# First-head row maxima among the last projections, and later memory units, in a two-layer attention trunk

## The chip, the cores and the metric

The kernel runs on one core of a Trainium2 chip. The metric is the time of one execution on the device in microseconds (us), the median of several runs; less is better. One execution was recorded by the hardware profiler, and the views of it are what is read below. The engines: PE (TensorE) multiplies, DVE (VectorE), ACT (ScalarE) and POOL (GpSimd) do the elementwise work, SP issues most loads. "bank" is one of the eight 512-column banks of PSUM, the only place PE writes to.

## The reference

A decoder trunk of two layers over 2048 tokens of width 1024. Layer A mixes tokens by multi-head latent attention, layer B by attention with forget gates; both have 12 causal heads and 4 heads that read 256 memory tokens.

```python
for i in range(DEPTH):                                   # A, then B
    hn = rms_norm(h, norm_pre[i])
    k_m, v_m = split(rms_norm(mem, mem_norm) @ w_mem_kv[i])
    if i % 2 == 0:
        c_q, c_kv, k_r, q_m, gate = split(hn @ w_in_a)
        main = mla(rms_norm(c_q) @ w_q_up, rms_norm(c_kv) @ w_kv_up, rope(...))   # causal softmax
    else:
        q, k, v, f_logit, q_m, gate = split(hn @ w_in_b)
        main = fox(q, k, v, cumsum(log_sigmoid(f_logit + b_f)))                  # causal softmax
    mem_out = softmax(q_m @ k_m.T * MEM_DIM**-0.5) @ v_m
    y = concat([main, mem_out]) * silu(gate)
    h = h + rms_norm(y @ w_out[i], norm_post[i])
```

## The kernel before

Every operand is split into a high and a low part, and a product is the sum of two or three matmuls of parts (`mm3`, L255). Intermediate results (q, k, v, gate, y) go through DRAM.

**The order of the program** (`trunk_kernel`): the projections of A; the up-projection `up_a` in four groups of 512 tokens; A's attention; `out_proj(0)`; `proj_b`, whose two last chunks (k and q of heads 8 to 11) run over the token groups in the order 1, 2, 3, 0; B's attention; `out_proj(1)`. `up_a` and `proj_b` are generators: at a `yield` they hand over to code that prepares the attention, so that this is placed among their last groups. Up to the attention the order on each engine comes from a list scheduler that goes by priority (`high_priority` puts work ahead) and by what its own model of the chip says is ready. `attention` itself is written out by hand, step by step (`manual_schedule`).

**Units and steps.** The attention is cut into units: one head and 512 queries (`Unit`, g = 0 to 3). A unit of a causal head needs first its row maxima (`max_closures`: q by k on PE at L1580, each 512 columns reduced on DVE at L1551 or, at the diagonal, L1583; 4 (g + 1) of them), then their negatives in a row of q (`nm`, `nm_row`, L1600 and L1601). Its steps then each make 1024 columns of logits (L1709), their exp on ACT (L1651), a high part on ACT (L202) and a low part on POOL (L224; on DVE where the step is narrow), and later the value products (L1725, 24 a step) and the division (`finish`, L1733 and L1738). A memory unit has two maxima (L1562) and one step.

**Memory units.** There are 16 in each layer. `MEM_EARLY` of them (6 in A, 8 in B) run among the last projections (`att_start`, `run_early`), `MEM_FIRST` (4, 4) at the head of the stream, and the rest follow, two per head (`MEM_AFTER`). The first causal head's k and v are loaded by `att_head`; all its maxima are made in the stream.

**The stream's planner** (`run_units`) keeps a list `maxq` of all maxima in order of units and, ahead of each step, lets out as many as a target in columns allows, at most `AHEAD` = 5 units ahead; half of them stand ahead of the step's logits on PE.

**Slots.** SBUF is cut into slots (A0 to A8, R0 to R4, S, G, Q), and a slot's next tenant waits until the last use of the one before. In `proj_b` the normalised input of group 1 lies in A4 and A5, of group 2 in A7 and A1, of group 3 in A2 and A8, of group 0 in A3 and A0. B's q of even heads lies in A3, of odd heads in A0. `up_a` stages its results in three tiles (`up_split`, L809 stores them) while its last group runs, and its banks are 4 and 7.

**The output projection** (`out_proj`): `z_prep` loads gate (L1195) and y (L1196) of 128 tokens, multiplies them on POOL (L1200), transposes on PE (L1204) and splits; the product is at L1229.

## Time and profile before

| | us |
|---|---|
| median of 3 runs | 2886.47 |
| lowest and highest run | 2885.28, 2890.05 |
| the profiled execution | 2885.39 |
| its span, first to last instruction | 2883.7 |

In the views, "out<-in" names tiles by the slots they lie in (bA is any of A0 to A8), and L255 is line 255 of the kernel. A stretch's PEclk is the clock granted to TensorE as a share of 2.4 GHz; 0.50 is its lower level, 1.2 GHz. A matmul's end is modelled, so busy times of neighbouring matmuls overlap slightly and distances between starts are the better price. A wait is put under the instruction that waited, behind the arrow what it waited for.

### The profile page before, as it was taken

The numbers are of one execution on the slowest core, as the hardware profiler recorded it, in microseconds if no ns is written. First come the engines' busy times: TensorE is split into PE (matmuls) and PEld (weight loads), VectorE is DVE, ScalarE is ACT, GpSimd is POOL, SyncE is SP. The second block draws the span as 40 slices with busy tenths as digits, with TensorE's granted clock in tenths as the row PEclk, the third lists the DMA queues.
The fourth block names the chain that finished last, engine by engine and source line by source line (L and its number), as shares of the span: only waits on it lengthen the run. The fifth ranks groups of instructions, "written<-read, shape, count | busy, mean of one in ns | idle before, by whom it ended". The sixth has DMA issues, their size and how long they took to land. (4 is left out here: it accounts for less than half of the span.)

```text
span 2883.7 us, 58600 instructions
## 1 busy us (share of the span) xinstructions
PE 2789.8 (97%) x24017; PEld 2379.9 (83%) x24017; DVE 1563.8 (54%) x3358; ACT 1323.0 (46%) x1867; POOL 1251.2 (43%) x838
## 2 busy tenths in 40 slices
PE   7999999879999999999999999999999999999998
PEld 6789998657888888878888997999767788887787
DVE  7522215467777777745463325310268788887343
ACT  4322123237778788852141010111137788888311
POOL 2110123346677777772101002310037788888431
PEclk9999999979999999999999999999979999999999
DMA  5343447763433343255443223861454454465453
GB/s 186 125 140 100 133 146 264 229 204 93 106 74 88 76 100 93 55 190 190 146 156 118 76 82 121 291 225 61 132 149 113 116 134 123 112 171 170 147 175 117
DMA packets 260933, 398.42 MB, mean 138 GB/s; under 512 B 24793, under 2 KB 140521, under 8 KB 260521
## 3 DMA queue, kind: packets, MB, share of 16 engines
q1 hardware_dynamic: 180112, 255.21, 31.4%
q10 hardware_dynamic: 79016, 138.27, 13.3%
q8 instruction: 189, 3.10, 0.5%
q0 software_dynamic: 1536, 1.18, 0.3%
q14 instruction: 80, 0.65, 0.1%
HBM read 238.13 MB, written 156.47 MB: 137 GB/s over the span
## 5 line engine op out<-in xcount | busy, mean ns | idle before, releaser
L224 POOL TENSOR_TENSOR bA<-bA,bA 128x1024 f16<-128x1024 f32 (+5 forms) x277 | 507.8, 1844 | 293.9 <-ACT bA L202 219.5
L255 PE MATMUL banks<-bR,bA 128*128 128x256 f32 (+3 forms) x4437 | 549.1, 286 | 1.1 <-DVE bQ L507 0.6
L255 PEld LDWEIGHTS banks<-bR,bA 128*128 128x128 f32 x4437 | 540.7, 188 | 6.5 <-ACT bG L505 0.9
L255 PE MATMUL banks<-bA,bR 128*128 128x512 f32 (+2 forms) x2208 | 514.6, 390 | 6.9 <-ACT bS L823 4.2
L1709 PE MATMUL banks<-bA,bA 96*128 96x512 f32 (+13 forms) x1820 | 483.9, 377 | 0.3 <-ACT bA L1651 0.2
L255 PEld LDWEIGHTS banks<-bA,bR 128*128 128x128 f32 x2208 | 403.4, 191 | 93.3 <-ACT bS L823 5.4
L1651 ACT ACTIVATE bA<-banks 128x1024 f32<-128x1024 f32 (+1 forms) x414 | 370.7, 895 | 182.9 <-PE banks L1709 156.9
L1551 DVE TENSOR_REDUCE mx<-banks 128x1 f32<-128x512 f32 x576 | 387.8, 685 | 108.3 <-PE banks L1580 105.6
L202 ACT ACTIVATE bA<-bA 128x1024 f16<-128x1024 f32 (+5 forms) x400 | 336.5, 848 | 95.8 <-DMA qrs<-bA 22.0
L1709 PEld LDWEIGHTS banks<-bA,bA 96*128 96x128 f32 (+3 forms) x1820 | 327.5, 193 | 43.1 <-ACT bA L1651 0.9
L1580 PE MATMUL banks<-bA,bA 76*128 76x512 f32 (+5 forms) x868 | 317.3, 406 | 17.6 <-DVE bA L1601 4.9
L209 POOL TENSOR_SCALAR bR<-bR 128x1024 fp32r<-128x1024 f32 (+3 forms) x50 | 61.5, 1230 | 410.8 <-PE banks L255 360.1
L1583 DVE CUSTOM_DVE_ANT_0 bA<-banks,bA 128x128 bf16<-128x128 f32 (+3 forms) x384 | 186.6, 486 | 76.7 <-PE banks L1580 66.1
L1229 PE MATMUL banks<-bA,bA 128*128 128x512 f32 x960 | 226.6, 392 | 0.0
L1725 PEld LDWEIGHTS <-bA 128*128 128x128 f16 x5928 | 198.9, 99 | 28.9 <-issue 16.5
L1229 PEld LDWEIGHTS banks<-bA,bA 128*128 128x128 f32 x960 | 178.6, 188 | 36.1
L1580 PEld LDWEIGHTS banks<-bA,bA 76*128 76x128 f32 (+1 forms) x868 | 164.2, 196 | 50.5 <-DVE bA L1601 7.6
L1709 PE MATMUL banks<-bR,bA 128*128 128x512 f32 (+6 forms) x620 | 201.6, 391 | 0.9 <-DVE bR L1601 0.9
L224 POOL TENSOR_TENSOR bR<-bR,bR 128x1024 f16<-128x1024 f32 (+2 forms) x74 | 159.9, 2161 | 81.7 <-ACT bR L202 49.5
L1200 POOL TENSOR_TENSOR bA<-bA 128x512 f32<-128x512 f32 x64 | 102.4, 1622 | 207.8 <-DMA bA<-gs 195.1
L224 POOL TENSOR_TENSOR bR<-bA,bR 128x1024 f16<-128x1024 f32 (+2 forms) x76 | 154.7, 2038 | 67.4 <-ACT bR L202 31.0
L505 ACT ACTIVATE bG<-banks 128x256 f32<-128x256 f32 x128 | 49.1, 385 | 277.2 <-PE banks L255 197.2
(228 smaller groups left out, 3638.7 us busy)
## 6 DMA issues: line engine op xcount, KB each, us to landing
bA<-qbs SPq DMA_DIRECT2D x65, 256.0 KB
bA<-in_x_dram SPq DMA_DIRECT2D x32, 512.0 KB
gs<-bG ACTq DMA_DIRECT2D x128, 128.0 KB
bA<-gs SPq DMA_DIRECT2D x32, 512.0 KB
bA<-ys SPq DMA_DIRECT2D x32, 512.0 KB
bA<-h SPq DMA_DIRECT2D x28, 512.0 KB
ks<-bA ACTq DMA_DIRECT2D x24, 512.0 KB
qs<-bA ACTq DMA_DIRECT2D x24, 512.0 KB
```

The costliest lines, as they stand in the source:

```text
L202: nc.scalar.activation(out, in_, AF.Copy, scale=scale)
L209: nc.gpsimd.tensor_scalar(out, in_, scale, 0.0, op0=ALU.mult, op1=ALU.add)
L224: e.tensor_tensor(out=out, in0=in_, in1=hi, op=ALU.subtract)
L255: nc.tensor.matmul(out, lhsT=a, rhs=b, start=start and i == 0, stop=stop and i == n - 1)
L1200: nc.gpsimd.tensor_tensor(out=gt[:, hs], in0=gt[:, hs], in1=yt[:, hs], op=ALU.mult)
L1229: nc.tensor.matmul(ps[:, ns], lhsT=a, rhs=b[:, ns], start=c == 0 and j == 0, stop=c == KC - 1 and j == 2)
L1551: nc.vector.tensor_reduce(out=to, in_=ps, axis=AX.X, op=ALU.max, negate=negate)
L1580: nc.tensor.matmul(ps, lhsT=q[0:qr, t * P:(t + 1) * P], rhs=k[0:kr, x:x + w], start=True, stop=True)
L1583: nc.vector.tensor_tensor_reduce(out=ap["mj"].next()[:, 0:w], in0=ps, in1=K.mqk[:, G - w:G], scale=1.0, scalar=-3.0e38, op0=ALU.add, op1=A ...
L1651: nc.scalar.activation(pf[:, 0:w], ps[:, 0:w], AF.Exp, scale=self.scale, bias=LOGP)
L1709: nc.tensor.matmul(ps[:, o:o + bw], lhsT=k[0:kr, (self.k0 + kt) * P:(self.k0 + kt + 1) * P], rhs=q[0:qr, q0:q0 + bw], start=i == 0 and not ...
L1725: nc.tensor.matmul(self.pv[:, t, 0:n], lhsT=p[:, o:o + P], rhs=v[:, kv, a:a + n], start=self.first, stop=False, skip_group_check=True)
```

## The change

It does six things.
- Early memory units: 6 to 2 in A, 8 to 4 in B. Units at the head of the stream: 4 to 0 in A, 4 to 2 in B; of B's two the maxima are made early too (`MEM_READY`). The others, 14 in A and 10 in B, stay two per head in the stream.
- The first causal head's maxima of g = 0 and 1 in A and of all four g in B are made in `att_head`, among the last projections, with their q loads (`q_row`, or `q_dma` in A) and the mask (`max_mask`). The planner counts them as done.
- In `proj_b` the yields come after the first and the third of the four last groups (before: after the second and the third), `att_head` before `att_start`, and two banks, 4 and 7, serve from the second group on (before: six banks, then three for the last two groups). Slots of B move to fit: head 0's k and v in A4 and A5, the memory's in A7, A1, A2 and A8, q of even heads in A6, of odd heads in A3.
- At the stream's end, when no maxima are left, the low part of a step is made on DVE right behind its high part.
- In `out_proj` the gate products of the first two tiles run on DVE, and the gain is loaded after the first tile's gate and y.
- q of the next two units is asked for ahead of every step.

```diff
--- before.py
+++ after.py
-MEM_EARLY = {0: 6, 1: 8}
-MEM_FIRST = {0: 4, 1: 4}
+ROWS_AHEAD = 600
+MEM_EARLY = {0: 2, 1: 4}
+ROWS_EARLY = {0: 2, 1: NG}
+MEM_READY = {0: 0, 1: 2}
+MEM_FIRST = {0: 0, 1: 2}
...
         prep(len(jobs) - 1)
         for g in (1, 2, 3, 0):
-            if g == 0:
+            if g == 2:
                 yield
-            elif g == 3:
+                env = (stp, self.banks(4, 7), hn)
+            elif g == 0:
                 yield
-                env = (stp, self.banks(4, 7, 1), hn)
             for k, (_, ms) in enumerate(last):
                 self.run_chunk(env, ms, W[len(jobs) - 2 + k], g)
...
+    def att_place(self, l):
+        if self.l != l:
+            self.ap, self.k_t, self.v_t, self.yt, self.l = {}, {}, {}, {}, l
+            self.ap["pm"], self.ap["ps"], self.ap["pv"] = self.banks(*((2, 3) if l == 0 else (1, 2, 3))), self.banks(5, 6), self.banks(0)
+        return self.ap
...
-            km, ph, pa, ymp, qq = B("A4", r=True), B("A5"), B("A7"), B("A1"), B("R4", r=True)
+            km, ph, pa, ymp, qq = B("A7", r=True), B("A1"), B("A2"), B("A8"), B("R4", r=True)
...
         first = [self.mem_units.pop(0) for _ in range(MEM_EARLY[l])]
-        for u in first:
+        ready = self.mem_units[:MEM_READY[l]]
+        for u in first + ready:
             u.q = ap["qq"].next()
         with self.tc.high_priority(offset=EARLY_AHEAD):
-            run_early(mem, first)
+            run_early(mem, first, ready)
...
-    def att_head(self):
-
-        l, B = self.l, self.box
-        self.v0 = B("A2" if l == 0 else "A8")
-        self.kv_place("0", B("A1" if l == 0 else "A2", r=True), self.v0)
+    def att_head(self, l):
+
+        B = self.box
+        self.att_place(l)
+        self.v0 = B("A2" if l == 0 else "A5")
+        self.kv_place("0", B("A1" if l == 0 else "A4", r=True), self.v0)
...
         self.head0 = Head(self, l, "mla" if l == 0 else "fox", 0)
         for _, f, _ in self.head0.prep():
             f()
+        self.ready = {}
+        if l:
+            self.qb_t = {}
+            self.qb_place("A6", 0)
+        mb = self.v0 if l else self.ap["mb"]
+        self.max_mask(mb, mb)
+        with self.tc.high_priority(offset=ROWS_AHEAD):
+            for g in range(ROWS_EARLY[l]):
+                u = self.ready[g] = Unit(self, l, self.head0, 0, g)
+                if l:
+                    u.q_row()
+                else:
+                    u.q = self.ap["qq"].next()
+                    u.q_dma()
+                for f, _ in u.max_closures():
+                    f()
+                u.nm()
+                u.nm_row()
+
...
+    def qb_place(self, slot, odd):
+
+        nb = DH + FB
+        box = self.box(slot, r=True)
+        for g in range(NG):
+            t = self.qb_t[g + NG * odd] = box.tile([nb, 2, G], F32R, name=f"qb{g}")
+            ind = self.v0.tile([FB, G], F32, name="ind")
+            self.nc.gpsimd.memset(ind, 1.0)
+            for lo_b, hi_b in ((-(NR + 2 * g), 0), (0, NR + 1 + 2 * g)):
+                self.nc.gpsimd.affine_select(out=ind, in_=ind, compare_op=ALU.is_ge, fill=0.0, base=lo_b + hi_b,
+                                             pattern=[[0, G]], channel_multiplier=1 if lo_b else -1)
+            self.nc.vector.tensor_copy(t[DH:nb], ind[:, None, :].to_broadcast([nb - DH, 2, G]))
...
-        self.kv_place("1", B("A3" if l == 0 else "A6", r=True), yb if l == 0 else B("Q"))
+        self.kv_place("1", B("A3" if l == 0 else "A0", r=True), yb if l == 0 else B("Q"))
...
+            self.qb_place("A3", 1)
...
         units = [mu.pop(0) for _ in range(min(MEM_FIRST[l], len(mu)))]
         for h, hd in enumerate(heads):
             for g in range(NG):
-                units.append(Unit(self, l, hd, hd.h, g))
+                units.append(self.ready[g] if h == 0 and g in self.ready else Unit(self, l, hd, hd.h, g))
...
-            late = mid + [later("A4", q1, k) for k in range(4)]
+            late = mid + [later("A7", q1, k) for k in range(4)]
...
-        zb, gb, xp = (B("A1", r=True), B("A2"), B("A8")) if l == 0 else (B("A1", r=True), B("A3"), B("A4"))
+        zb, gb, xp = (B("A1", r=True), B("A2"), B("A8")) if l == 0 else (B("A8", r=True), B("A3"), B("A7"))
...
-        gain = xp.tile([P, D], F32, name="ogain")
-        self.bcast_row(gain, i["norm_post"][l])
...
-                nc.gpsimd.tensor_tensor(out=gt[:, hs], in0=gt[:, hs], in1=yt[:, hs], op=ALU.mult)
+                (nc.vector if t < 2 else nc.gpsimd).tensor_tensor(out=gt[:, hs], in0=gt[:, hs], in1=yt[:, hs], op=ALU.mult)
...
         nxt = z_prep(0)
+        gain = xp.tile([P, D], F32, name="ogain")
+        self.bcast_row(gain, i["norm_post"][l])
...
                 o.pv_steps([(s, box)])
             o.finish()
-    for u in objs[:3]:
+    both = objs + ready
+    for u in both[:3]:
         u.q_dma()
-    for u in objs[:2]:
+    for u in both[:2]:
         rows(u)
     for k, u in enumerate(objs):
-        if k + 3 < len(objs):
-            objs[k + 3].q_dma()
-        if k + 2 < len(objs):
-            rows(objs[k + 2])
+        if k + 3 < len(both):
+            both[k + 3].q_dma()
+        if k + 2 < len(both):
+            rows(both[k + 2])
...
+        if o.has_row:
+            at += sum(c for _, c in o.max_closures())
+            maxq.extend(late)
+            late.clear()
+            continue
...
+    done = sum(need[u] for u, o in enumerate(objs) if o.has_row)
...
-            if u > main and not (st["done"] + c <= target and u <= main + AHEAD):
+            if objs[u].hd.idx > cur[main] + 1 or u > main and not (c <= target and u <= main + AHEAD):
...
+        q_ahead(u + 2, u)
         close()
-        todo = advance(u, min(t * rate + lead, RUNUP * (t + 4 * G) + need[0]))
+        todo = advance(u, min(t * rate + lead, RUNUP * (t + 4 * G) + need[0] + done))
...
-        o.flow(s, box)
+        o.flow(s, box, st["k"] == len(maxq) and not todo)
         if before:
             before[0].flow_lo(before[1])
         before = None
+        if st["k"] == len(maxq) and not todo:
+            o.flow_lo(box)
+            box["dve"] = False
...
+    def q_row(self):
+
+        K, h, g = self.K, self.h, self.g
+        if self.mx_ops:
+            return
+        kb, nb = self.hd.kt[1], DH + FB
+        qb = self.qb = K.qb_t[g + NG * (h % 2)]
+        K.load_r(qb[0:DH], K.qbs[h // 2][(h % 2) * DH:(h % 2) * DH + DH, :, g * G:(g + 1) * G])
+        self.mx_ops = ((qb[:, 0], nb), (kb, nb))
+        self.nmrow, self.at = qb[DH:DH + NR, 1], DH
...
         nc.scalar.activation(pf[:, 0:w], ps[:, 0:w], AF.Exp, scale=self.scale, bias=LOGP)
         K.hi("act", ph[:, 0:w], pf[:, 0:w])
-        if w > G:
+        box["dve"] = w <= G or last
+        if not box["dve"]:
             K.lo("pool", pl[:, 0:w], pf[:, 0:w], ph[:, 0:w])
 
     def flow_lo(self, box):
         w = box["w"]
-        if w <= G:
+        if box["dve"]:
             self.K.lo("dve", box["pl"][:, 0:w], box["pf"][:, 0:w], box["ph"][:, 0:w])
...
     next(pb)
+    K.att_head(1)
+    next(pb)
     K.att_start(1)
-    next(pb)
-    K.att_head()
     drain(pb)
     K.attention()
```

## Rows read from the trace of the kernel before

**Rows 1.** The page: busy time, share of the span and instructions.

```profile
PE 2789.8 (97%) x24017; PEld 2379.9 (83%) x24017; DVE 1563.8 (54%) x3358; ACT 1323.0 (46%) x1867; POOL 1251.2 (43%) x838
```

**Rows 2.** Stretches: window, length, busy by engine (instructions), PEclk, DMA share, GB/s.

```profile
550.00:610.00 60.00, 48.62 (x263) 37.02 (x261) 34.61 (x53) 20.97 (x34) 22.12 (x22) 0.94 0.80 252
610.00:660.00 50.00, 36.72 (x182) 26.19 (x183) 33.00 (x74) 17.89 (x24) 18.14 (x15) 0.56 0.47 133
...
1100.00:1200.00 100.00, 99.51 (x1239) 83.30 (x1236) 73.29 (x164) 80.12 (x100) 77.70 (x42) 1.00 0.33 82
1254.00:1262.00 8.00, 4.42 (x97) 3.73 (x94) 3.10 (x4) 2.42 (x5) 6.27 (x5) 1.00 0.83 301
2127.00:2172.00 45.00, 39.34 (x215) 28.07 (x214) 37.04 (x77) 17.96 (x21) 19.27 (x17) 0.58 0.52 132
2172.00:2310.00 138.00, 131.47 (x1682) 106.24 (x1681) 105.33 (x247) 109.24 (x120) 104.38 (x50) 0.96 0.44 113
2400.00:2500.00 100.00, 98.73 (x1314) 80.90 (x1311) 83.49 (x194) 87.27 (x99) 84.63 (x40) 1.00 0.47 125
2654.00:2687.00 33.00, 25.98 (x358) 20.97 (x355) 5.61 (x9) 22.62 (x26) 30.75 (x17) 0.84 0.61 224
```

**Rows 3.** PE's waits, 550 to 660: waiter, releaser, us, times, longest.

```profile
PE banks L1562 <- DMA bA<-qms: 5.6, 3, 3.6
PE banks L1709 <- ACT bR L1691: 4.9, 1, 4.9
...
PE banks L1580 <- DMA bA<-qrs: 2.6, 1, 2.6
```

**Rows 4.** ACT's waits, 550 to 645, the longest.

```profile
ACT bA L202 <- DMA qrs<-bA: 15.0, 3, 7.2
```

**Rows 5.** PE in order of time: start, us, line, shape, count.

```profile
2113.21 0.40 PE L1709 MATMUL banks<-bA 128*128 128x512 f32 x1
...
2114.37 1.55 PE L255 MATMUL banks<-bA,bR 128*128 128x512 f32 x6
...
2117.59 5.01 PE L255 MATMUL banks<-bA,bR 128*128 128x512 f32 x21
2122.44 0.39 PE L1709 MATMUL banks<-bR,bA 128*128 128x512 f32 x1
```

**Rows 6.** SP in order of time, first v loads of A.

```profile
602.97 10.87 SPq L1458 DMA_DIRECT2D bA<-vs  x4
```

**Rows 7.** A stretch of B's projections, and a DVE group in it.

```profile
2036.00:2128.00 92.00, 92.00 (x517) 71.33 (x516) 32.36 (x55) 23.06 (x35) 13.85 (x14) 1.00 0.49 147
...
L224 DVE TENSOR_TENSOR bA<-bA,bA 128x512 f16<-128x512 f32 x6 | 4.2, 693 | 11.0 <-ACT bA L202 11.0
```

**Rows 8.** DVE: the maxima of the whole span; two copies in order of time.

```profile
L1551 DVE TENSOR_REDUCE mx<-banks 128x1 f32<-128x512 f32 x576 | 387.8, 685 | 108.3 <-PE banks L1580 105.6
...
2139.36 3.22 DVE L1108 CAST bA<-bA 12x1024 fp32r<-12x1024 f32 x2
```

**Rows 9.** PE's waits, 2127 to 2310, the longest.

```profile
PE banks L1580 <- DMA bA<-qbs: 4.1, 2, 2.6
```

**Rows 10.** The stream's end in B, in order of time.

```profile
2654.10 4.25 POOL L224 TENSOR_TENSOR bA<-bA,bA 128x1024 f16<-128x1024 f32 x2 [0.64 <-POOL bG L224]
2659.29 2.51 POOL L1200 TENSOR_TENSOR bA<-bA 128x512 f32<-128x512 f32 x2 [0.94 <-DMA bA<-ys]
...
2664.10 1.02 ACT L1651 ACTIVATE bA<-banks 128x1024 f32<-128x1024 f32 x1 [3.36 <-POOL bA L224]
2665.15 1.06 ACT L202 ACTIVATE bA<-bA 128x1024 f16<-128x1024 f32 x1
...
2648.87 1.63 PE L1725 MATMUL banks<-bQ,bA 128*128 128x65 f16 x48
```

**Rows 11.** DVE in order of time, the same shape twice.

```profile
664.93 0.57 DVE L224 TENSOR_TENSOR bQ<-bA,bG 128x256 f16<-128x256 f32 x1
...
2684.55 1.81 DVE L224 TENSOR_TENSOR bA<-bA,bA 128x256 f16<-128x256 f32 x1 [13.04 <-ACT bA L202]
```

More of the change, by code (lines that the diff above doesn't have):

```diff
@@ L197, in __init__ @@
         self.owed = 0.0
+        self.l = None
     def hi(self, eng, out, in_, scale=1.0):
@@ L1032, in att_start @@
         ap["qq"] = Turn(*(Later(lambda b=b, k=k: b.tile([P, 2, G], F32R, name=f"qq{k}")) for k, b in enumerate(qqs)))
-        ap["ymp"], ap["sp"] = ymp, sp
+        ap["ymp"], ap["sp"], ap["mb"] = ymp, sp, pa
         ap["ym"] = Turn(*(ymp.tile([P, 4, 2 * DH], F32, name=f"ym{k}") for k in range(4)))
         ap["vrm"] = Turn(vrp.tile([P, MEMH * NMEM // P, DH], F32, name="vrm"))
-        ap["pm"], ap["ps"], ap["pv"] = self.banks(2, 3), self.banks(5, 6), self.banks(0)
-        self.l, self.yt = l, {}
         self.k_ones("m")
@@ new lines, in max_mask @@
+    def max_mask(self, mb, jb):
+        mqk = self.mqk = mb.tile([P, G], BF16, name="mqk")
+        self.ap["mj"] = Turn(jb.tile([P, G], BF16, name="mj"))
+        self.nc.gpsimd.memset(mqk, 0.0)
+        self.nc.gpsimd.affine_select(out=mqk[:, G - P:G], in_=mqk[:, G - P:G], compare_op=ALU.is_ge, fill=NEG, base=0,
+                                     pattern=[[-1, P]], channel_multiplier=1)
+    def qb_place(self, slot, odd):
[9 more added lines that the diff above has]
+            self.nc.vector.tensor_copy(t[DH:nb], ind[:, None, :].to_broadcast([nb - DH, 2, G]))
@@ L1084, in attention @@
         gb, fewer = B("G"), None
-        mb, jb = (v0, yb) if l == 0 else (ap["sp"],) * 2
-        mqk = self.mqk = mb.tile([P, G], BF16, name="mqk")
-        ap["mj"] = Turn(jb.tile([P, G], BF16, name="mj"))
-        nc.gpsimd.memset(mqk, 0.0)
-        nc.gpsimd.affine_select(out=mqk[:, G - P:G], in_=mqk[:, G - P:G], compare_op=ALU.is_ge, fill=NEG, base=0,
-                                pattern=[[-1, P]], channel_multiplier=1)
         more = (v0, yb, gb, ap["sp"]) if l == 0 else (ap["ymp"], gb, v0, v0)
@@ L1098, in attention @@
             ap["qa"] = Turn(*(Later(lambda k=k: qa.tile([P, G], F32R, name=f"qa{k}")) for k in range(4)))
-            qb = B("A3", r=True), B("A0", r=True)
-            self.qb_t = [qb[j // NG].tile([nb, 2, G], F32R, name=f"qb{j}") for j in range(2 * NG)]
-            for g in range(NG):
-                ind = v0.tile([FB, G], F32, name="ind")
-                nc.gpsimd.memset(ind, 1.0)
-                for lo_b, hi_b in ((-(NR + 2 * g), 0), (0, NR + 1 + 2 * g)):
-                    nc.gpsimd.affine_select(out=ind, in_=ind, compare_op=ALU.is_ge, fill=0.0, base=lo_b + hi_b,
-                                            pattern=[[0, G]], channel_multiplier=1 if lo_b else -1)
-                for j in (g, g + NG):
-                    nc.vector.tensor_copy(self.qb_t[j][DH:nb], ind[:, None, :].to_broadcast([nb - DH, 2, G]))
+            self.qb_place("A3", 1)
         heads = [self.head0] + [Head(self, l, "mla" if l == 0 else "fox", h) for h in range(1, HEADS)]
@@ L1137, in attention @@
             ts = early if u.kind == "mem" or l == 0 and u.hd.idx < MORE_Q else late if k > free else mid
-            u.q = min(ts, key=lambda q: used.get(q, -1))
+            u.q = u.q or min(ts, key=lambda q: used.get(q, -1))
             used[u.q] = k
         W = self.W = {}
-        slots = ("A4", "A4", "A5", "A5", "A7", "A7", "R0", "S") if l == 0 else ("R2", "R3", "R4", "S", "A2", "A2", "A8", "A8")
+        slots = ("A4", "A4", "A5", "A5", "A7", "A7", "R0", "S") if l == 0 else ("R2", "R3", "R4", "S", "A4", "A4", "A5", "A5")
         wb = {}
@@ L1211, in out_proj @@
         nxt = z_prep(0)
+        gain = xp.tile([P, D], F32, name="ogain")
+        self.bcast_row(gain, i["norm_post"][l])
+        if l == 0:
+            self.xbox = B("A6")
+            gpre = self.gpre = self.xbox.tile([P, D], F32, name="ogpre")
+            self.bcast_row(gpre, i["norm_pre"][1])
         for t in range(NT):
@@ L1255, in out_proj, with run_early @@
                 yield
-def run_early(mem, objs):
+def run_early(mem, objs, ready):
     K = mem.K
@@ L1297, in run_units @@
     n = len(objs)
-    maxq, late = [], []
+    maxq, late, at = [], [], 0
     for u, o in enumerate(objs):
+        if o.has_row:
[3 more added lines that the diff above has]
+            continue
         cols = 0
         for f, c in o.max_closures():
-            maxq.append((u, f, c))
+            at += c
+            maxq.append((u, f, at))
             cols += c
@@ L1307, in run_units @@
         late.append((u, o.nm_row, 0))
-    maxq.append(late.pop())
+    maxq.extend(late)
     steps = [(u, s, max(b[1] + b[3] for b in s)) for u, o in enumerate(objs) for s in o.steps()]
-    need = [0] * n
-    for u, f, c in maxq:
-        need[u] += c
+    cur = [1] * n
+    for u, o in enumerate(objs):
+        cur[u] = o.hd.idx or cur[max(u, 1) - 1]
+    need = [sum(c for _, c in o.max_closures()) for o in objs]
     width = [0] * n
@@ L1336, in run_units @@
     aux.sort(key=lambda x: (x[0], x[1]))
-    st = dict(k=0, done=0, dma=0)
+    st = dict(k=0, dma=0)
     def run_aux(t, head=-1):
@@ L1367, in advance @@
             todo.append(f)
-            st["done"] += c
             st["k"] += 1
@@ L1639, in main_closures, with flow @@
         return out
-    def flow(self, blocks, box):
+    def flow(self, blocks, box, last):
         K, nc, ap = self.K, self.K.nc, self.K.ap
@@ L1753, in trunk_kernel @@
     next(up)
-    K.att_head()
+    K.att_head(0)
     drain(up)
```

28 lines of the change are left out of this document (10 added, 18 removed).

## The prediction

> **What bounds the kernel now.** First the page's line of busy times: PE is busy for 97% of the span [rows 1], so look for what PE loses, not for what the other engines do. The second view is the table of stretches: for each stretch the PE busy time times the granted clock is the work at 2.4 GHz that was done in it, and the length less that is loss. In the two attention streams almost nothing is lost: 100 - 99.51 = 0.5 us of 100 in layer A, 100 - 98.73 = 1.3 us of 100 in layer B [rows 2]. There PE itself sets the pace, and work put into a stream costs what it takes on PE. The loss sits at the seams [rows 2]:
> - 550 to 610, last group of A's up-projection: 60 - 48.62 x 0.94 = 14.3 us.
> - 610 to 660, the way into A's stream: 50 - 36.72 x 0.56 = 29.4 us.
> - 1254 to 1262, A's stream into the output projection: 8 - 4.42 = 3.6 us.
> - 2127 to 2172, the way into B's stream: 45 - 39.34 x 0.58 = 22.2 us.
> - 2172 to 2310, B's first head and a half: 138 - 131.47 x 0.96 = 11.8 us.
> - 2654 to 2687, the end of B's stream: 33 - 25.98 x 0.84 = 11.3 us.
>
> Together 92.6 us. The product takes the mean clock for the busy time, so each is an estimate. Most of the two big ones is clock: granted 0.56 and 0.58, that is mostly the 1.2 GHz level, after PE had begun to wait. Everything the change does is at these seams.
>
> **The price of a memory unit.** The third view is PE's order of time late in B's projections. One cycle from one unit to the next lasts 2122.44 - 2113.21 = 9.23 us and holds 27 projection matmuls [rows 5]; the run of 21 takes from 2117.59 to 2122.44, so 0.231 us each and 6.24 us for the 6 + 21. The unit itself is 9.23 - 6.24 = 3.0 us of PE. In A eight units leave the seam (six early and four first become two and none), in B six (eight and four become four and two): 24 and 18 us of PE. All of it comes back in the streams at 3.0 us each, at full clock; nothing is saved by the move as such. What counts is whether the loss at the seam shrinks.
>
> **A, the way into the stream (29.4 us).** PE waits here for q of memory units (5.6 us), for q rope of the first head (2.6 us), and 4.9 us for an exp [rows 3]; the exp stood on ScalarE behind a copy that waited for a staging tile's store to land, as the 15.0 us of such waits show [rows 4]. After: the first head's first two units bring their four q loads, their 12 maxima and two negated-row steps forward beside the last q projections, behind the k loads of that head on SP. The two DMA waits go. The staging wait stays, because the three staging tiles stay: 4.9 us. A shorter stretch at 1.2 GHz behind it: 10 us, costing 5. A new burst: the planner lets about nine maxima into the first step, 9 x 0.685 = 6.2 us of VectorE [rows 8] against 9 x 0.231 = 2.1 us of PE with three banks between them: 3 us after the logits of that step are taken off. Left 13, bounds 5 (no pause, so no fall of the clock) and 24 (only the waits for memory q go). Gain 16.
> Against it: the units that leave were also filler. Between 550 and 610 PE waits for banks behind the same stores, and four early units of 3.0 us stood in those holes or would have to: 0 to 12 us of new holes; the 12 maxima, 12 x 0.231 = 2.8 us, fill some. I take 3, near the low end, because 48.62 of 60 us were busy, so most units displaced projection work rather than holes. First values: the v loads of the first head are issued from 602.97 on, 10.87 us long [rows 6], while the stream would now reach its first value product near 620; that can cost up to 8 us and is inside the upper bound. **A net: 13 us.**
>
> **A, the end (3.6 us).** POOL's two gate products for the first tile stand in PE's way here; at B's end such a pair takes 2.51 us [rows 10]. On VectorE the nearest row is 0.69 us for 128x512 with two operands [rows 7], 1.4 us a pair. The broadcast of the gain is queued behind the first tile's loads instead of ahead of them. The last low parts go to VectorE. Gain 2.4, bounds 0 and 3.6.
>
> **B, the way into the stream (22.2 us).** Between 2036 and 2128 VectorE is busy for 32.36 of 92 us while PE is full [rows 7]; then the seam has both the first head's maxima and the eight copies of the indicator rows, two of which together took 3.22 us [rows 8], on a full VectorE: 37.04 of 45 us [rows 2]. After: the 40 maxima of the first head (4 + 8 + 12 + 16) move to where VectorE is free, 40 x 0.685 = 27.4 us, and four of eight copies with them; 32 + 27 + about 6 still leaves a third of the 92 us. On PE they are 40 x 0.231 = 9.2 us, paid either way. SP issues the first head's k and v loads after the first of the four last groups instead of after the third; POOL builds its masks there, idle for 78 of 92 us [rows 7]. The four early units now wait for the third group's slots, so they have one group, 4 x 24 x 0.231 = 22 us, to stand beside: four units, four results, the same one-to-one cycle as in [rows 5]. Left: 3 us for the last unit's exp, split and product, 2 us of first logits without values, 2 us of clock: 7, bounds 3 and 18 (the chains start late and two units stick out at 1.2 GHz). Gain 15.
>
> **B, the first heads (11.8 us).** The wait for q, 4.1 us [rows 9], goes, since q is asked for at every step. New: with a head of maxima in hand the planner issues none for about ten steps. Such a step is 4 x 0.231 + half of the 48 value products of 1.63 us = 1.74 us on PE, 1.02 + 1.06 = 2.08 us on ScalarE, and 4.25 / 2 = 2.13 us on POOL [rows 10]: POOL leads by 0.39, some 4 us over ten steps. Gain 1 taken with the first logits, bounds -3 and 6.
>
> **B, the end (11.3 us).** No maxima are left after 2654, and POOL carries all low parts and the gate products too, 2.51 us per tile [rows 10]; the exp then waits 3.36 us for POOL [rows 10]. After: VectorE takes the low parts. Nine full steps and some short ones on ScalarE are 9 x 2.08 + 2.4 = 21 us, with a last low part and products 26 of the present 33. Price of a 128x1024 low part on VectorE: between four times 0.57 us for 128x256 with POOL quiet, and four times 1.81 us with POOL busy [rows 11]; I take the low end, since POOL has little left, and 2.3 us is already near ScalarE's 2.08. That gains 6. Against it: the output projection's first tiles lie in slot A3, which so far held the q of even heads, free after head 10; now it holds the q of odd heads, and the loads of the first tile wait for the last logits of head 11. At A's end, where these loads land about as late, 3.6 us are lost [rows 2]; with the gate products on VectorE I take 2. Gain 4, bounds -1 and 9.
> The 0.57 and the 1.81 us for one shape agree with a rule of the Trainium skill, GPSIMD Engine Reference, section 1 Specifications: POOL shares its SBUF interfaces with VectorE, and instructions with two SBUF inputs contend. By that rule the remaining gate products on POOL would stretch two or three of the low parts by about 1.2 us each, an estimate from the rows, and the end would gain 1 instead of 4.
>
> **Sum.** 13 + 2.4 + 15 + 1 + 4 = 35.4 us. The profiled execution took 2885.4 us, 1.7 of it outside its span of 2883.7; it lies 1.1 us under the median of 2886.5. So 2886.5 - 35.4 = 2851.
>
> **Rivals.**
> 1. *The seams close.* Left 5 in A's way in with no new holes, 2 in B's, 4 in B's first heads, 3 at the end, 1 at A's end: gains 24.4 + 20 + 8 + 8 + 2.6 = 63, 2823. For: the waits named are all ended by what the change moves. Against: the staging waits of [rows 4] are untouched.
> 2. *The filler was needed.* In A 24 left and 12 us of new holes: 29.4 - 24 - 12 = -7, the rest as forecast (22.4): gain 15, 2871. For: 14.3 us are lost there with the filler in place.
> 3. *The rows do not come early.* The list order puts the maxima behind the projections, because k or q of the first head lands late: no gain at B's way in and start, 5 in A, 6.4 at the ends: 2875. Against: k and q of that head were written long before.
> 4. *Slower: B's two banks.* From the second of the four last groups on, results alternate between two banks (before six, then three). If VectorE, its queue full of reductions, takes more than the 24 x 0.231 = 5.5 us of one result to clear the other bank, PE stops at each of 12 results. At 1.5 us each that is 18 us, and such stops are what preceded the low clock in [rows 2]; half of these 12 x 5.5 = 66 us at 1.2 GHz adds 33. With no gain in B's way in and start: 2886.5 + 51 - 19.4 = 2918. Against: a third of VectorE is free by the sum above, and clearing needs one 0.69 us subtraction [rows 7] behind a copy. It decides from a delay of 5.5 us on.
>
> **How the numbers follow.** Chances: forecast 0.47 (2838 to 2864), rival 1 0.15, rival 2 0.17, rival 3 0.10, rival 4 0.11. The range 2823 to 2876 takes in the first three and most of rival 3, and leaves out rival 4 and the lower half of rival 1. A measurement of this kernel tells about 0.2%, 6 us, from no change. Rivals 2 and 3 reach toward no change in part, and rival 4's small end too: faster 0.85, within 0.06, slower 0.09.
>
> **What would show it.** Right: granted clock above 0.8 in the 50 us ahead of each stream's first steady steps; maxima of the first head among projection matmuls; no wait of PE for memory q; VectorE doing 128x1024 low parts at the end, with no wait of the exp for POOL. Wrong: PE waiting for projection banks in B's last groups, a low clock there, or PE waiting for the first head's v.

## The result, and the profile after

The changed kernel takes **2920.05 us** (median of 4 runs, 2914.51 to 2922.13) against 2885.88 beside it: ratio 1.0115, 95% interval 1.0102 to 1.0129. It is slower by 34 us where 35 us of gain were forecast. The profiled execution has a span of 2919.4 us. A profile shows one execution, and those of one kernel can differ by 10 us and more (of the kernel with layer A's early maxima alone, below, two of twelve took 2880 to 2881 us and ten 2888 to 2893, and its profile is of one of the two), so kernels are compared by medians and intervals, and stretches only say where.

First the four long stretches in which the two kernels differ. Columns as in [rows 2]: window, length, busy time by engine (instructions), PEclk, DMA share, GB/s. The kernel before:

```profile
500.00:800.00 300.00, 268.33 (x2252) 213.38 (x2252) 203.28 (x405) 159.96 (x208) 157.40 (x98) 0.90 0.54 156
800.00:1240.00 440.00, 438.07 (x5366) 365.88 (x5362) 322.24 (x723) 352.48 (x435) 336.38 (x180) 1.00 0.33 81
2100.00:2200.00 100.00, 93.55 (x732) 70.20 (x731) 73.04 (x157) 46.91 (x56) 43.95 (x29) 0.81 0.55 141
2200.00:2500.00 300.00, 291.95 (x3851) 238.85 (x3851) 239.15 (x543) 252.99 (x284) 242.93 (x115) 0.98 0.45 120
```

The changed kernel:

```profile
500.00:800.00 300.00, 278.73 (x2413) 224.31 (x2413) 201.13 (x417) 168.62 (x217) 166.92 (x100) 0.90 0.52 146
800.00:1240.00 440.00, 429.64 (x5118) 355.88 (x5117) 315.90 (x702) 338.07 (x413) 324.06 (x173) 0.98 0.34 84
2100.00:2200.00 100.00, 86.98 (x663) 64.28 (x662) 56.70 (x113) 44.75 (x54) 40.66 (x27) 0.81 0.35 103
2200.00:2500.00 300.00, 285.58 (x3564) 232.74 (x3564) 225.10 (x505) 234.24 (x260) 224.14 (x107) 0.94 0.45 115
```

The loss by the prediction's own sum (length less PE busy time times clock) goes from 58.5 to 49.1 us in A's seam, from 1.9 to 19.0 in A's stream, from 24.2 to 29.5 in B's seam and from 13.9 to 31.6 in B's stream. (The clock's two decimals leave an error of up to 2 us in a row of 440 us, and the mean clock hides in which part of a row PE was busy. The sums compare kernels; they are no exact account.) So A's seam gained, B's seam did not, and each of the two streams loses some 17 us more. The four together are 30.7 us of the 34.

The changed kernel's rows that answer to [rows 2] in A's way in and at the end of B's stream:

```profile
550.00:610.00 60.00, 50.21 (x234) 39.40 (x234) 37.74 (x69) 20.25 (x33) 25.36 (x26) 0.82 0.81 252
610.00:660.00 50.00, 45.42 (x279) 33.69 (x279) 30.06 (x74) 23.37 (x29) 19.95 (x11) 0.64 0.44 115
...
2690.00:2723.00 33.00, 27.16 (x400) 21.62 (x399) 18.34 (x26) 24.59 (x28) 5.95 (x3) 0.93 0.63 227
```

They lose 18.8, 20.9 and 7.7 us, where it was 14.3, 29.4 and 11.2 (33 - 25.98 x 0.84; the prediction has 11.3).

PE's waits in the changed kernel (waiter, releaser, us, times, longest); 550 to 660, then 800 to 1240, then 2200 to 2500:

```profile
PE banks L1633 <- DVE mx L1636: 5.5, 3, 2.5
...
PE banks L1633 <- DMA bA<-qrs: 5.9, 3, 3.6
PE banks L1653 <- DVE nmw L1604: 2.3, 1, 2.3
...
PE banks L1633 <- DMA bA<-qbs: 10.2, 5, 2.9
```

The waits for the memory units' q and the first q rope of [rows 3] are gone from A's seam, as forecast (0.3 us is left of the rope's). The same kind of wait, a maximum (L1633) that stands behind the load of its q, is now in the middle of both streams; in B it grew from the 4.1 us of [rows 9]. Here is one in order of time, the changed kernel in A: SP issues the load, PE's last logits ahead of it, PE's next maximum.

```profile
1011.61 0.39 PE L1633 MATMUL banks<-bA,bA 96*128 96x512 f32 x1
1011.80 0.52 SPq L1018 DMA_DIRECT2D bA<-qs  x1
1011.84 1.11 PE L1763 MATMUL banks<-bA,bR 128*128 128x512 f32 x4
1012.38 0.59 SPq L1018 DMA_DIRECT2D bA<-qrs  x1
...
1016.54 1.19 PE L1633 MATMUL banks<-bA,bA 96*128 96x512 f32 x2 [3.59 <-DMA bA<-qrs]
```

The load is issued only at 1011.80, and PE has some 1 us of logits left before it must have the data. Why so late? The planner's rule: a unit's q may be loaded only when no earlier unfinished unit uses the same tile. While memory units are left in the stream, B's causal units share four tiles (`qa`), and so do A's from head index `MORE_Q` = 6 on. `free`, the index of the last memory unit plus 7, ends that. The change moves the memory units later in the stream, so `free` goes from 28 to 48 in A and from 22 to 38 in B. This is theory Q. Its rivals: M, a memory unit in the stream is simply dearer than 3.0 us; P, the new limits on how far the maxima run ahead; R, the early rows upset the stream's order.

### The profile page after: what moved, and what is told of

It is laid out like the page before. It is cut to its first block, busy times and chain, and to the rows that moved or that the text cites. A ratio compares the mean times of both kernels' runs of the same rounds, so it can differ in the third digit from the quotient of the medians.

```text
span 2919.4 us, 58593 instructions
## 1 busy us (share of the span) xinstructions
PE 2812.6 (96%) x24017; PEld 2397.9 (82%) x24017; DVE 1575.7 (54%) x3376; ACT 1324.2 (45%) x1859; POOL 1215.0 (42%) x824
## 3 DMA queue, kind: packets, MB, share of 16 engines
q10 hardware_dynamic: 79016, 138.27, 13.1%
## 4 chain that ended last, share of the span: by engine, by line
PE 72%; DMA 12%; issue 8%; DVE 4%; POOL 1%; ACT 1%; SPq 0%; ACTq 0%; DVEq 0%; POOLq 0%
PE banks L259 23%; PE banks L1763 16%; PE banks L1261 12%; PE banks L1779 10%; PE banks L1633 7%; DMA bA<-kbs 1%; DMA bA<-qbs 1%; DMA qs<-bA 1%; DMA ws<-bA 1%; PE banks L1230 1%; PE banks L350 1%; DMA bA<-vs 1%; DMA bR<-qms 1%; DMA bR<-in_w_in_b_dram 1%; DVE bA L228 1%
## 5 line engine op out<-in xcount | busy, mean ns | idle before, releaser
L228 POOL TENSOR_TENSOR bA<-bA,bA 128x1024 f16<-128x1024 f32 (+4 forms) x268 | 489.7, 1837 | 276.0 <-ACT bA L206 205.0
L1763 PE MATMUL banks<-bA,bA 100*128 100x512 f32 (+5 forms) x1872 | 511.0, 382 | 0.0
L1704 ACT ACTIVATE bA<-banks 128x1024 f32<-128x1024 f32 (+1 forms) x421 | 377.2, 896 | 202.0 <-PE banks L1763 169.2
L1763 PEld LDWEIGHTS banks<-bA,bA 100*128 100x128 f32 (+2 forms) x1872 | 347.0, 198 | 43.9 <-ACT bA L1704 0.2
L1633 PE MATMUL banks<-bA,bA 76*128 76x512 f32 (+5 forms) x904 | 340.1, 413 | 38.6 <-DMA bA<-qbs 13.6
L1633 PEld LDWEIGHTS banks<-bA,bA 76*128 76x128 f32 (+1 forms) x904 | 174.2, 198 | 75.1 <-issue 18.9
L1763 PE MATMUL banks<-bR,bA 128*128 128x512 f32 (+7 forms) x568 | 201.0, 403 | 2.0 <-ACT bA L1704 1.9
L1226 POOL TENSOR_TENSOR bA<-bA 128x512 f32<-128x512 f32 x56 | 91.1, 1647 | 230.7 <-DMA bA<-gs 199.3
L509 ACT ACTIVATE bG<-banks 128x256 f32<-128x256 f32 x128 | 49.1, 385 | 277.8 <-PE banks L259 176.6
L228 POOL TENSOR_TENSOR bR<-bA,bR 128x1024 f16<-128x1024 f32 (+2 forms) x69 | 141.8, 2056 | 74.7 <-ACT bR L206 35.1
L206 ACT ACTIVATE bS<-banks 128x512 fp32r<-128x512 f32 (+2 forms) x72 | 42.1, 584 | 265.8 <-PE banks L259 219.3
```

What stands on the lines that cost most here:

```text
L206: nc.scalar.activation(out, in_, AF.Copy, scale=scale)
L228: e.tensor_tensor(out=out, in0=in_, in1=hi, op=ALU.subtract)
L509: nc.scalar.activation(st[:, 0:2 * P], ps[:, 0:2 * P], AF.Silu)
L1226: (nc.vector if t < 2 else nc.gpsimd).tensor_tensor(out=gt[:, hs], in0=gt[:, hs], in1=yt[:, hs], op=ALU.mult)
L1633: nc.tensor.matmul(ps, lhsT=q[0:qr, t * P:(t + 1) * P], rhs=k[0:kr, x:x + w], start=True, stop=True)
L1704: nc.scalar.activation(pf[:, 0:w], ps[:, 0:w], AF.Exp, scale=self.scale, bias=LOGP)
```

## The experiments

**Few tiles in the kernel before, more in the changed one.** The first holds the kernel before to four tiles for as long as the changed one (four units sooner by index, since fewer units are interleaved):

```
-        free = max([k for k, u in enumerate(units) if u.kind == "mem"], default=0) + AHEAD + 2
+        free = 44 if l == 0 else 34
```

> The kernel before, in which the causal units are held to four q tiles for as long as in the changed kernel (to unit 44 of layer A, unit 34 of layer B); its memory units, its way in and its order stay. Theory Q: the loss of the changed kernel's streams appears here, 2912 to 2924 us. Rivals M and P: 2884 to 2890 us, since neither a memory unit nor a limit is moved.

Measured: 2927.69 us, ratio 1.0139 [1.0120, 1.0159], 41 us slower with no unit moved; by its profile A's stream loses 24.0 us instead of 1.9, B's 34.7 instead of 13.9. The other direction, with eight tiles for every causal unit of B:

```
-MORE_Q = 6
+MORE_Q = 9
...
-            early, mid = few + [later(x, q2, k) for x in ("R2", "R3") for k in range(2)], ap["qa"].tiles
-            late = mid + [later("A7", q1, k) for k in range(4)]
+            early, mid = few + [later("R3", q2, k) for k in range(2)], ap["qa"].tiles + [later("R2", q1, k) for k in range(4)]
+            late = ap["qa"].tiles + [later("A7", q1, k) for k in range(4)]
```

> The changed kernel with more q tiles while memory units are left in the stream: in layer A every causal head may use the early set, in layer B a causal unit has eight tiles from the first head on instead of four (four taken from the memory units' set). Nothing else differs. Theory Q (the stream lost 16.5 us in A and 20 us in B because a unit's q is loaded only when one of four tiles comes free, and PE stands behind that load and falls to the lower clock): 2884 to 2892 us. Rival M (each memory unit placed in the stream costs more than its PE time, whatever the tiles): 2914 to 2922 us. Rival P (the limits that the change puts on how far the maxima run ahead): 2914 to 2922 us.

Measured: 2887.09 us, ratio 1.0001 [0.9990, 1.0013]; 33 us of the 34 are back. The waits of the kernel before with few tiles, 800 to 1240, then 2200 to 2500:

```profile
PE banks L1580 <- DMA bA<-qrs: 13.6, 5, 4.9
...
PE banks L1580 <- DMA bA<-qbs: 14.4, 7, 3.2
```

The same two stretches of the changed kernel with more tiles:

```profile
800.00:1240.00 440.00, 429.55 (x5183) 356.48 (x5182) 324.75 (x703) 341.32 (x417) 326.19 (x174) 0.98 0.35 85
2200.00:2500.00 300.00, 295.88 (x3940) 240.87 (x3939) 247.94 (x556) 258.64 (x288) 248.15 (x117) 1.00 0.49 125
```

B's stream loses 4.1 us instead of 31.6: there Q is shown in both directions, and P falls, since its limits are in this kernel. In A the q waits are gone, but the row is the same as before, 19.0 us. So A's stream has a second cause behind the first; it comes below.

**Was the wait in the kernel before too?** Eight tiles in B, by the same lines (with slot A4 for A7), nothing else:

> The kernel before with eight q tiles in layer B from the first head on, nothing else. Theory Q: the q waits that the kernel before shows between 2172 and 2310 go, 2874 to 2881 us. Rival (they are covered by other lateness there): 2884 to 2888 us.

Measured: 2879.62 us, ratio 0.9975 [0.9964, 0.9985]. The q wait was a real cost before the change; what removes it is tiles.

**The first head's early maxima.** `ROWS_EARLY` set to 0 in both layers of the changed kernel:

> The changed kernel without the first head's maxima among the last projections, in both layers; the memory units stay where the change puts them. Theory Q: the streams lose the same 36 us, and the two seams give back what the early maxima brought or took (8 gained in A, 7 lost in B): 2912 to 2932 us. Rival R (the early rows upset the stream's order): 2880 to 2895 us.

Measured: 2905.4 us, ratio 1.0064 [1.0046, 1.0082]. Neither theory's range (2912 to 2932, 2880 to 2895) holds it: the streams lose as in the changed kernel (18.6 and 33.5 us by its rows), so R falls, but leaving out the early maxima gave 15 us. So four kernels with more tiles, which differ in `ROWS_EARLY` alone:

> The changed kernel with more q tiles and without the first head's maxima among the last projections. The two causes add if they are separate: the changed kernel 2920, less the 15 us that leaving out the early rows gave, less the 28 us by which more tiles relieved layer B's stream: 2868 to 2882 us, faster than the kernel before. Rival (the early rows help once the tiles do not bind): 2885 to 2900 us.

> As the one before, but layer A keeps its two early row maxima; layer B has none. If the early rows cost in both layers: 3 to 6 us above the one without rows. If only layer B's forty maxima cost (its memory rows stand behind them): within 2 us of the one without rows.

> More q tiles, and the first head's early maxima in layer B alone; layer A has none. With the kernels that have them in both layers (2887), in layer A alone (2889) and in neither (2877) this completes the four. If it is layer A's early maxima that cost: 2874 to 2880 us. If layer B's cost too: 2882 to 2890 us.

| early maxima | median us | ratio | 95% interval |
|---|---|---|---|
| none | 2877.10 | 0.9966 | 0.9953 to 0.9979 |
| B's forty | 2883.48 | 0.9974 | 0.9961 to 0.9987 |
| A's two units | 2889.47 | 1.0003 | 0.9991 to 1.0016 |
| both (above) | 2887.09 | 1.0001 | 0.9990 to 1.0013 |

(The run with B's forty had 2890.18 us for the kernel before beside it, so compare ratios.) A's early maxima cost 0.3%, 8 to 11 us; B's cost nothing that these runs can tell. Of A's cost the profiles show a part: the row of 500 to 800 loses 42.5 us with none and 43.6 with B's alone, 51.5 with A's alone and 52.0 with both. Most of the difference lies from 610 to 660 (10.8 and 13.1 us lost without A's, 20.2 and 20.4 with them), and it is clock. From 630 to 640, without early maxima and with A's alone:

```profile
630.00:640.00 10.00, 9.57 (x109) 7.38 (x105) 8.84 (x19) 6.72 (x8) 5.18 (x4) 1.00 0.49 122
630.00:640.00 10.00, 9.86 (x56) 7.48 (x56) 4.30 (x11) 4.16 (x4) 4.84 (x3) 0.53 0.98 230
```

PE is nearly full in both, at full clock in the first and mostly at 1.2 GHz in the second. What keeps the clock down longer is open: the kernel with three units to a head, below, has no early maxima either and is granted 0.65 there.

**Layer A's second cause.** With more tiles and no early rows, the memory units of A back in their old places:

```
-MEM_EARLY = {0: 2, 1: 4}
+MEM_EARLY = {0: 6, 1: 4}
...
-MEM_FIRST = {0: 0, 1: 2}
+MEM_FIRST = {0: 4, 1: 2}
```

> More q tiles, no early rows, and layer A's memory units back in their old places: six on the way in, four at the head of the stream; layer B as in the changed kernel. If filler on the way in and units late in the stream only trade places: within 4 us of the one with two early units. If the A stream's 13 us come from memory units in heads 4 to 6: 4 to 13 us below it. If the two early units alone made the gain of layer A's seam: 5 to 12 us above it.

Measured: 2878.84 us, ratio 0.9969 [0.9959, 0.9979], the same as with the units moved (0.9966). Its rows of A's seam and stream:

```profile
500.00:800.00 300.00, 269.12 (x2278) 215.65 (x2277) 201.18 (x404) 159.14 (x206) 156.84 (x97) 0.89 0.53 152
800.00:1240.00 440.00, 438.06 (x5335) 365.46 (x5331) 323.72 (x721) 352.31 (x436) 332.80 (x177) 1.00 0.33 81
```

The same of the kernel without early maxima whose units are moved:

```profile
500.00:800.00 300.00, 276.85 (x2483) 223.33 (x2482) 202.89 (x426) 173.64 (x222) 170.60 (x103) 0.93 0.52 147
800.00:1240.00 440.00, 429.60 (x5199) 356.57 (x5198) 324.25 (x696) 342.14 (x419) 321.14 (x172) 0.98 0.35 86
```

Units moved back: seam 60.5, stream 1.9. Units moved on: seam 42.5, stream 19.0. What the seam gains in these two profiles, 18 us, the stream loses, 17. The longest wait in that stream, from the changed kernel with more tiles in order of time:

```profile
1017.34 2.14 POOL L228 TENSOR_TENSOR bR<-bR,bR 128x1024 f16<-128x1024 f32 x1
1017.55 8.46 DVE L228 TENSOR_TENSOR bR<-bA,bR 128x256 f16<-128x256 f32 x1
...
1019.45 1.44 POOL L228 TENSOR_TENSOR bA<-bA,bA 128x256 fp32r<-128x256 f32 x2
...
1020.86 2.12 POOL L228 TENSOR_TENSOR bR<-bA,bR 128x1024 f16<-128x1024 f32 x1
...
1027.28 0.60 PE L1779 MATMUL banks<-bQ 128*128 128x65 f16 x8 [6.16 <-DVE bA L1792]
```

One low part of 128x256 takes 8.46 us on DVE; the division (L1792) is queued behind it, and PE's value product waits 6.16 us for the bank. POOL subtracts beside it almost without a gap, stream low parts and the halves of the output weights (128x256, fp32r). Two runs on that. In the first the units stand three to a head, so that the last is in the fifth head:

```
-MEM_AFTER = {0: (2, 3), 1: (1, 3)}
+MEM_AFTER = {0: (1, 2, 3), 1: (1, 3)}
```

> More q tiles, no early rows, and in layer A three memory units after each head's units instead of two, so that the last of them stands in the fifth head, ahead of the splitting of the output weights on POOL. If the one 8.46 us subtraction on DVE (128x256, beside five subtractions on POOL without a gap) comes of weight splitting and memory units together: it is gone, with the 6.1 us wait of PE behind it, and the time is 2866 to 2873 us. If a memory unit in the stream is dear wherever it stands: 2875 to 2882 us, with the loss between 700 and 1000.

Measured: 2875.51 us, ratio 0.9968 [0.9956, 0.9980]. The instruction, the wait and the loss of the row are gone (3.0 us are left), with the same units in the stream, so M falls as a general price:

```profile
800.00:1240.00 440.00, 437.01 (x5346) 363.21 (x5343) 324.38 (x710) 351.32 (x431) 328.16 (x175) 1.00 0.35 84
```

But the median is 1.6 us from the kernel with two to a head, within the intervals; in its profile the seam lost 49.8 instead of 42.5 us, and of the 9 us by which the row gained more than that the medians show 1.6. So the rows say where A's stream loses, and the times do not show that this loss has a price. The other run takes weight splitting off POOL, for the first two chunks:

```
-            self.lo("pool", lo, w, h)
+            self.lo("pool" if c else "dve", lo, w, h)
```

> More q tiles, no early rows; the low halves of the first two chunks of layer A's output weights are subtracted on DVE instead of POOL, sixteen instructions of 128x256 in all. If POOL without a gap is what held the DVE subtraction: no 8.46 us instruction, 2868 to 2874 us. If DVE's own load holds PE there: 2877 us or more.

Measured: 2885.7 us, ratio 0.9992 [0.9977, 1.0007], by the median 9 us above the kernel without the edit (0.9966, and the two intervals overlap: five of its twelve executions took 2873 to 2878 us, seven 2885 to 2891). In its profile, which is of one of the seven, the stretch 800 to 1240 loses 28.4 us instead of 19.0, and 7 of the 9 us more lie between 880 and 940 (13.4 against 6.0). An 8.45 us instruction stands at 1021.54 as before: those two chunks are split around 900, and the stretch hit at 1021 still has POOL's. The run gives no sign that VectorE is a better place for them, and leaves the cause open. Such an instruction stands at this place in seven of the eight profiles whose layer A has more tiles and its units moved on, two to a head; the eighth (below, units back in B) is without it. So a late memory unit beside a full POOL is where it appears, but what exactly starts it is not settled.

Nor is it the whole loss. The eighth profile's row, and PE's longest wait in it:

```profile
800.00:1240.00 440.00, 435.62 (x5280) 361.50 (x5277) 323.66 (x708) 349.22 (x426) 325.41 (x174) 0.99 0.36 87
...
PE banks L1653 <- DVE nmw L1604: 2.2, 1, 2.2
```

It still loses 8.7 us, 5.6 of them between 885 and 925, where PE stands 2.2 us behind a memory unit's own maxima and is at the lower clock after it. The changed kernel, with more tiles or without, loses 5.7 us there, the kernel with three to a head 0.1. Between 1005 and 1045 the loss is 8.3 us in the changed kernel (q waits), 9.4 with more tiles (the long subtraction), 0.2 in the eighth profile. So of the 17 us some 6 stand at the first place and 8 to 9 at the second.

**B's seam.** The forty maxima went to where the prediction put them: 30 of them stand among the projections, and PE is full until 2122. The four memory units did not: their first rows (L1615) come behind the last maximum. The changed kernel, PE in order of time:

```profile
2127.57 0.56 PE L1633 MATMUL banks<-bA,bA 76*128 76x384 f32 x1 [0.94 <-DVE mx L1604]
2128.79 0.80 PE L1633 MATMUL banks<-bA,bA 76*128 76x512 f32 x1 [0.66 <-DVE mx L1636]
2129.53 0.79 PE L1615 MATMUL banks<-bA 64*128 64x256 f32 x2
```

Its stretches there:

```profile
2030.00:2122.00 92.00, 92.00 (x405) 74.80 (x404) 33.65 (x70) 9.83 (x17) 10.63 (x20) 1.00 0.45 144
...
2122.00:2130.00 8.00, 4.51 (x12) 1.97 (x10) 7.78 (x16) 1.74 (x2) 3.45 (x6) 0.86 0.23 89
2130.00:2140.00 10.00, 8.15 (x22) 4.89 (x22) 8.38 (x15) 2.63 (x4) 2.39 (x4) 0.50 0.08 20
2140.00:2150.00 10.00, 10.00 (x66) 7.11 (x66) 5.96 (x11) 3.91 (x5) 3.81 (x3) 0.50 0.31 87
```

Both groups take their PSUM banks from one ring of three. Own banks for each, two ahead of the first head's maxima and one ahead of the memory units, on top of more tiles:

```
+        if l:
+            self.ap["pm"] = self.banks(1, 2)
...
+        if l:
+            ap["pm"] = self.banks(3)
```

> The one with more q tiles, and in layer B the first head's maxima use two PSUM banks and the four early memory units the third, so that the memory units' rows need not wait for the last of the forty maxima in one ring of three. If that ring is what held the memory rows back until 2129.5: 4 to 10 us below the one with more q tiles alone, and memory rows ahead of the last maxima. If the order of priorities holds them: the same within 2 us.

Measured: 2908.64 us, ratio 1.0073 [1.0056, 1.0090], 21 us worse than with more tiles alone. The memory rows still follow the last maximum, and that comes 14 us later than with more tiles alone (2124.36 there): with two banks PE waits ten times, 6.6 us in all, for VectorE to reduce a maximum (L1637 is L1633 here, L1619 is L1615):

```profile
2138.59 0.79 PE L1637 MATMUL banks<-bA,bA 76*128 76x512 f32 x1 [0.91 <-DVE mx L1608]
2141.53 0.79 PE L1619 MATMUL banks<-bA 64*128 64x256 f32 x2 [0.67 <-DVE bA L1658]
```

So the shared ring is not what puts the memory rows last; what it costs, this run cannot tell, because it also took a bank from the maxima. Then the order: memory units first.

```
-    K.att_head(1)
     next(pb)
     K.att_start(1)
+    K.att_head(1)
```

> The changed kernel with more q tiles; in layer B the four early memory units are set up ahead of the first head's maxima instead of behind them, both at the place where the memory units were. If the maxima, first in order on PE and DVE, hold the memory rows back until after the last projection and so lengthen the seam: memory rows before 2121, the maxima between and behind them, layer B's seam 5 to 9 us shorter, 2878 to 2882 us. If the seam's loss is set by the clock, whichever of the two comes first: 2885 to 2890 us.

Measured: 2896.43 us, ratio 1.0040 [1.0025, 1.0054]. The first memory rows are at 2075 now, well ahead of 2121, but only 6 of the 40 maxima are issued ahead of the last nine projections, and 34 lie behind them:

```profile
2123.72 2.31 PE L259 MATMUL banks<-bA,bR 128*128 128x512 f32 x9
...
2127.35 1.04 PE L1633 MATMUL banks<-bA,bA 76*128 76x512 f32 x2 [0.72 <-DVE mx L1636]
...
2142.94 7.66 PE L1633 MATMUL banks<-bA,bA 76*128 76x512 f32 x12
```

B's row of 2100 to 2200 loses 35.3 us here, 31.1 with the maxima first. Order isn't it either: whichever group comes second lies behind the last projection, at the low clock (0.54 granted from 2126 to 2160). Last, B's units back in their old places, with no early maxima and more tiles (`MEM_EARLY` 8, `MEM_READY` 0, `MEM_FIRST` 4 for B):

> More q tiles, no early rows, and layer B's memory units back in their old places: eight on the way in, four at the head of the stream; layer A as in the changed kernel. If the four units moved into layer B's stream are free there once the tiles do not bind, and the seam does not need them: within 3 us of the one with four early units (2874 to 2880 us). If they filled the seam: 4 to 12 us less. If they lengthened it: 4 to 12 us more.

Measured: 2875.66 us, ratio 0.9962 [0.9948, 0.9976]. Within the intervals that is the kernel with four early units; by its profile B's seam loses 21.9 against 28.5 us.

**Put together:** more tiles, no early maxima, A three to a head, B's units in their old places.

> What the runs so far favour, put together: more q tiles, no early rows, layer A with two early memory units and three per head in the stream, layer B with eight early and four at the head of its stream as before the change. If the gains of the two layers add: 2868 to 2874 us, the fastest so far. If they are the same few us of run to run change: 2874 to 2878 us.

Measured: 2873.6 us, ratio 0.9957 [0.9945, 0.9969], 12 us under the kernel before and the lowest median of all; its interval overlaps those of its parts. It keeps of the change A's fewer early units, the two ends, and what was rearranged in B's last projections. Eight tiles in B alone gave the kernel before 7 of the 12 us (0.9975), and the two intervals overlap, so what the change itself adds is some 5 us that the runs do not show for certain.

## Why the prediction was wrong

**The step that failed first: "The wait for q, 4.1 us [rows 9], goes, since q is asked for at every step."** Asking oftener gets nothing where the tile is not free. That wait rose to 10.2 us in the row of B's stream, and with the clock behind it the stream lost 31.6 instead of 13.9 us. Forecast +1 with a bound of -3, measured some -18; with eight tiles the same stream loses 4.1, a gain of 10. The line that decides, `free`, was in the code that the prediction read, and the wait was in its rows. It should have asked when the tile of that q comes free, and what the moved units do to `free`.

**"All of it comes back in the streams at 3.0 us each, at full clock; nothing is saved by the move as such."** In A the 17 us that the stream lost were in no term and no rival: a wait for a memory unit's own maxima near 900, and near 1016 q (5.9 us of waits in all) or, without that, one slow subtraction. Such a wait can cost PE more than itself: from 2130 to 2150 above PE is at half clock after a hole though it is nearly full, and so it is after a q wait in B, for example the 1.78 us that ended at 2337.74. The changed kernel, in order of time:

```profile
2332.88 0.53 SPq L1018 DMA_DIRECT2D bA<-qbs  x1
...
2337.74 0.47 PE L1633 MATMUL banks<-bA,bA 76*128 76x512 f32 x1 [1.78 <-DMA bA<-qbs]
```

Its stretch behind that:

```profile
2340.00:2350.00 10.00, 10.00 (x70) 8.23 (x70) 4.72 (x12) 4.96 (x6) 4.60 (x3) 0.52 0.37 88
```

4.8 us more were lost in those 10 us, with PE busy throughout.

**A, the way in: right in kind, 13 forecast, 9 measured** (58.5 to 49.1 us over 500 to 800; the way in itself 29.4 to 20.9 where 16 were to go, and 4.5 us of new loss ahead of it where 3 were set). The DMA waits went, and PE's 4.9 us behind an exp too. The wait for staged results stayed, as forecast, and reached PE by way of the early maxima instead, 5.5 us in three waits. One of them: ScalarE's high part at 607.20 had waited 7.76 us for a store, and behind it stand, in order of time,

```profile
607.86 0.69 DVE L228 TENSOR_TENSOR bA<-bA,bA 128x512 fp32r<-128x512 f32 x1 [3.87 <-ACT bA L206]
...
610.28 1.22 PE L1633 MATMUL banks<-bA,bA 96*128 96x512 f32 x2 [2.02 <-DVE mx L1636]
```

But the early maxima had no part in the gain: of the kernels with more tiles, those without them lose less here (42.5 against 52.0 us). "Gain 16" was put to the wrong edit; it came with the units that left, as the kernel with the units moved back shows (60.5). Rival 2, the filler was needed, did not come.

**B, the way in: gain 15 forecast, 5 lost.** That the rows fit beside the projections was right (30 of 40; VectorE 33.65 of 92 us, "still leaves a third" was cautious). "Four units, four results, the same one-to-one cycle" was wrong: none stood beside a result. The bound written for that ("the chains start late and two units stick out at 1.2 GHz", 18 us left) was on the low side: all four stuck out. Rival 4, the two banks, did not come: PE is full until 2122. So slower came by a mechanism that was no rival, and that this rival's 2918 us lie near the measured 2920 is chance.

**B, the end: right.** Gain 4 forecast, 11.2 - 7.7 = 3.5 measured. The low parts on VectorE took 1.23 us, less than the 2.3 taken. The 0.57 us of [rows 11] from which that came was no price with POOL quiet: a POOL subtraction ran until 665.21 beside it, and with POOL quiet the shape takes 0.42. None of these low parts was stretched by POOL, whose last work in the 33 us ends at 2696.6 (5.95 us busy), and whose remaining gate products came later. So the lower gain of 1 us by the Trainium skill's rule did not come, and its condition was not met. The late loads of the first tile cost about the 2 us set against them. The changed kernel, in order of time:

```profile
2699.44 0.42 DVE L228 TENSOR_TENSOR bG<-bA,bA 128x256 f16<-128x256 f32 x1
...
2707.10 1.23 DVE L228 TENSOR_TENSOR bA<-bA,bA 128x1024 f16<-128x1024 f32 x1 [0.16 <-ACT bA L206]
...
2719.43 1.29 DVE L1226 TENSOR_TENSOR bA<-bA 128x512 f32<-128x512 f32 x2 [1.47 <-DMA bA<-ys]
...
2720.18 1.25 PE L1230 MATMUL banks<-idf,bA 128*128 128x128 f32 x8 [2.44 <-DVE bA L1226]
```

**A, the end: wrong by 3 us.** Gain 2.4 forecast; PE still waits for the gate products, on VectorE now, 2.0 us where it was 1.8, and no gain is seen (from 1250 to 1275 3.6 us were lost, and 4.5 now).

The range ended at 2876 because every term was costed at a seam; the work that left the seams had one price, and it was read where PE was full and no load was late.

## What to carry to other kernels

Before moving filler into a stream that runs without loss, find what else its position decides there: here the index of the last filler unit set for how long B's causal units had half of their q tiles. When a wait in the trace is for a DMA, read back to its issue and ask what released the buffer; a planner that asks sooner, or an order with more lead, does nothing if the buffer is what is late. And price a wait in a full stream with the clock that follows it, not by its own length.

## What the runs showed of the hardware that was not expected

- The clock stayed at its 1.2 GHz level (0.50 granted from 2130 to 2150, 0.52 from 2340 to 2350) with PE busy for 8.15 to 10.00 of 10 us, so filling PE after a hole doesn't give the lost time back at once.
- The same subtraction of 128x256 took DVE 0.42 us with POOL quiet (2699.44 above), 0.57 beside the end of a POOL instruction, 1.81 beside POOL [rows 11], and 8.46 beside POOL almost without a gap, while 128x1024 with POOL quiet took 1.23. The rule of the Trainium skill that the prediction cited (GPSIMD Engine Reference, section 1 Specifications: interfaces shared with VectorE) agrees in kind; the size is a measurement of these runs, and why it came in some kernels with the same code and not in another is open.
